# The opening of a two-layer decoder trunk in a fixed order: x in 8 pieces in turn with the weights, a first unit in halves

## The chip, the cores and the metric

The kernel runs on one core of a Trainium2 chip. A core has a matrix engine (TensorE, PE in the profile, with its weight loads shown as PEld), a vector engine (DVE), a scalar engine (ACT), GpSimd (POOL) and an engine that mostly issues transfers (SyncE, SP). Each engine takes its instructions in the order in which they stand in its own stream, and they wait for each other by semaphores. The metric is the device time of one execution in microseconds; the kernel before takes 2566.13 us (median of 3 runs, 2565.7 to 2566.15).

## What is computed

256 tokens of 2048 channels pass through two layers. Layer 0 has a Mamba-2 state-space mixer, layer 1 a short gated convolution, and each is followed by a gated feed-forward with a causal convolution. All is float32. Cut to what the opening computes:

```python
def rms_norm(x, w):
    y = x * lax.rsqrt(jnp.mean(x * x, axis=-1, keepdims=True) + EPS)
    return y * w

def ssd_mixer(u, w_in, conv_w, conv_b, dt_bias, a_log, d_skip, norm_w, w_out):
    zxbcdt = u @ w_in                                  # u: 256 x 2048, w_in: 2048 x 10304
    z, xbc, dt_raw = jnp.split(zxbcdt, [D_INNER, D_INNER + SSM_CONV_DIM], axis=-1)
    xbc = jax.nn.silu(causal_dwconv(xbc, conv_w, conv_b))
    xs, bm, cm = jnp.split(xbc, [D_INNER, D_INNER + SSM_BC_DIM], axis=-1)
    dt = jax.nn.softplus(dt_raw + dt_bias)
    ...

for i in range(2):
    x = x + mixer_i(rms_norm(x, mix_norm_w[i]))        # ssd_mixer, then short_conv_mixer
    x = x + conv_ffn(rms_norm(x, ffn_norm_w[i]))
return rms_norm(x, final_norm_w)
```

## The kernel before

**Tiling.** Channels lie on the 128 partitions and tokens along the free dimension, so x is kept as eight pairs of 128 channels (`xp`, `x_pair`), each 128 x 2 x 256. Float32 products are made from split operands: every weight and every activation is divided into a high and a low part, and three products are summed, high times high, high times low and low times high. A *unit* of weights is 2 x 128 rows by 512 columns (`KU`, `COLS`, 512 KB). For each unit ACT casts it to its high part `wh` (L260) and DVE subtracts to get the low part `wl` (L261). The activations' parts lie side by side in an `hl` tile, made by `split_pair` (ACT L206, DVE L207); the first norm's per-channel weight is multiplied in there.

**Streams.** `stream` (L274) makes 512 output columns from all 16 row blocks, eight units in turn. For each unit it goes through four column tiles t and two row blocks k; each of these eight pairs (t, k) has three products, 24 per unit (L293, L294, L297 where one sum is kept in 256 columns). A stream fills two PSUM tiles (`main`, of which there are three) and then evacuates them. The order of streams is B and C of four groups, then for each group xs and z, then the output product, and so on. Weights move on through four raw buffers (`rawpool`) and four buffers each of `wh` and `wl` (`WB`); other PSUM results use two `aux` tiles.

**The opening.** Rows of x are loaded on SP in eight transfers of 256 KB, each 128 tokens by 512 channels (`load_x`, L81). `x_pair` (L367), called ahead of each unit of the first stream, transposes two channel blocks on PE (four transposes, L375), copies them out of PSUM (L380: DVE for the first two pairs, ACT for the others), splits them and adds a sum of squares on DVE (L388). After the eighth pair it also transposes parameter rows 1 to 3 and makes the norm's per-token factor: reduction (L396), Newton steps (`rsqrt`, L158 to L166), a diagonal (L174), a broadcast by four products (L176) and a copy into `r0` (L400). Every evacuation of the first streams multiplies by `r0` (L314), and a convolution along tokens follows (L328, L330). Between the first and second stream stand the products for dt (64 small products, L449), its softplus, running sums, and the row `cs_d` that is written to DRAM (L495) and read back as `cbc` for the decays (L542). Parameter rows are loaded on ACT's queue and transposed (`load_params`, L136); row 0 holds the mixer norm's weights that the first splits need.

**What sets the order.** The program is traced in the order of the code, and a planner then arranges each engine's stream by its own forecast of when each instruction is ready; priority goes by the traced order, and tiles are handed out as buffers come free. `tc.high_priority(0)` moves the splits of the first eight units ahead (L259). Nine products of ones (L97), read by nobody, run before x arrives.

Of the kernel before, what the change touches and what calls it, by code (L numbers as in the profile page):

```python
# [16 lines left out]
P = 128  # L17
T = 256
# [21 lines left out]
def trunk_kernel(ctx, tc, a, out):  # L40
# [35 lines left out]
    tokpool = start.enter_context(tc.tile_pool(name="tokpool", bufs=2))  # L76
    xt = []
    for c in range(2):
        xt.append(tokpool.tile([P, D], F32, tag="xt", name=uid("xt")))

    def load_x(q):  # L81
        for c in range(2):
            nc.sync.dma_start(
                out=xt[c][:, q * 512 : (q + 1) * 512],
                in_=a["x"][0, c * P : (c + 1) * P, q * 512 : (q + 1) * 512],
            )

# [48 lines left out]
    def load_params(i):  # L136
        n = min(P, total - i * P) if i else n_mix
        rt = small.tile([P, P], F32, tag="prow", name=uid("prow"))
        for off, r in pieces[i]:
            nc.scalar.dma_start(out=rt[off : off + r.shape[0], :], in_=r)  # L140
        ps = aux()
        nc.tensor.transpose(ps[:, :n], rt[:n, :], ident[:n, :n])
        nc.vector.tensor_copy(prm[i][:, :n], ps[:, :n])
# [6 lines left out]
    load_params(0)  # L150

# [1 line left out]
    def rsqrt(v, n):  # L153
        """v**-0.5 for v > 0, [P, n], from an integer seed by Newton's method."""
        r = small.tile([P, n], F32, tag="rs_r", name=uid("rs_r"))
        t = small.tile([P, n], F32, tag="rs_t", name=uid("rs_t"))
        sh = small.tile([P, n], I32, tag="rs_i", name=uid("rs_i"))
        ts(out=sh, in0=v.bitcast(I32), scalar1=1, scalar2=None, op0=ALU.logical_shift_right)  # L158
        ts(
            out=r.bitcast(I32), in0=sh, scalar1=-1.0, scalar2=float(0x5F3759DF),  # L160
            op0=ALU.mult, op1=ALU.add,
        )
        for _ in range(3):
            stt(out=t, in0=r, scalar=-0.5, in1=v, op0=ALU.mult, op1=ALU.mult)
            tt(out=t, in0=t, in1=r, op=ALU.mult)
            stt(out=r, in0=t, scalar=1.5, in1=r, op0=ALU.add, op1=ALU.mult)  # L166
        return r

    def bcast_tok(r):
        """r [tokens, 2] -> PSUM [P, 256], the same row on every partition."""  # L170
        dg = small.tile([P, 2, P], F32, tag="dg", name=uid("dg"))
        ps = aux()
        for c in range(2):
            ts(out=dg[:, c, :], in0=ident, scalar1=r[:, c : c + 1], scalar2=None, op0=ALU.mult)  # L174
        for c in range(2):
            mm(ps[:, c * P : (c + 1) * P], ones, dg[:, c, :], start=True, stop=True)  # L176
# [21 lines left out]
    def split_pair(hl, src, wname=None, k0=0):  # L198
        """hl[:, j] = [high | low] parts of src[:, j] (times a per-channel weight)."""
# [4 lines left out]
        for j in range(2):  # L204
            w = pcol(wname, k0 + j)
            act(hl[:, j, 0:T], src[:, j, :], AF.Copy, scale=w)  # L206
            stt(  # L207
                out=hl[:, j, T : 2 * T], in0=src[:, j, :], scalar=w,
                in1=hl[:, j, 0:T].bitcast(F32), op0=ALU.mult, op1=ALU.subtract,
            )  # L210

# [35 lines left out]
    units = []  # L247
    taken = [0]

    def load_unit():  # L250
        w, c0, kc = plan[len(units)]
        raw = rawpool.tile([P, KU, COLS], F32, tag="raw", name=uid("raw"))
        nc.sync.dma_start(
            out=raw,
            in_=w[kc * P : (kc + KU) * P, c0 : c0 + COLS].rearrange("(k p) n -> p k n", p=P),
        )
        wh = wpool.tile([P, KU, COLS], F32R, tag="wh", name=uid("wh"))
        wl = wpool.tile([P, KU, COLS], F32R, tag="wl", name=uid("wl"))
        with tc.high_priority(0 if len(units) < NKD // KU else None):  # L259
            nc.scalar.copy(wh, raw)  # L260
            tt(out=wl, in0=raw, in1=wh.bitcast(F32), op=ALU.subtract)  # L261
# [12 lines left out]
    def stream(c0, hls, kcs, evac, one=False, before=None):  # L274
        """Products of COLS columns of w with the split activations; evac(pair, psum).

        The sum lies in columns 0..T of psum, or with one unset in two parts, 0..T and T..2T.
        """
        pts = [psm.tile([P, 2, 512], F32, tag="main", name=uid("main")) for _ in range(2)]
        n = len(kcs)  # L280
        for u in range(0, n, KU):
            if before is not None:
                before(u)
            wh, wl = weight_unit(c0, kcs[u], WB - 1 if before is None else 1)
            for t in range(4):
                o = pts[t // 2][:, t % 2, :]
                for k in range(KU):
                    i = u + k
                    hl = hls[i // 2][:, i % 2, :]
                    lw = slice(t * P, (t + 1) * P)  # L290
                    first, last = i == 0, i == n - 1
                    if one:
                        mm(o[:, 0:T], wh[:, k, lw], hl[:, 0:T], start=first, stop=False)  # L293
                        mm(o[:, 0:T], wh[:, k, lw], hl[:, T : 2 * T], start=False, stop=False)  # L294
                    else:
                        mm(o, wh[:, k, lw], hl, start=first, stop=False)  # L296
                    mm(o[:, 0:T], wl[:, k, lw], hl[:, 0:T], start=False, stop=last)  # L297
# [22 lines left out]
    def conv(s, width, wname, nk, k0, bname=None, tag="tp", pool=None):  # L320
        """Causal depthwise conv along tokens; channels k0*128.. of nk*128."""
# [15 lines left out]
    class Norm:  # L337
        """Sum of squares over channels, gathered pair by pair."""
# [24 lines left out]
    xp, xhl = [], []  # L363
    ss = small.tile([P, 2, 4], F32, tag="ss", name="ss")
    first = {}

    def x_pair(u):  # L367
        m = u // KU
        if m % 2 == 1 and m < 7:
            load_x(m // 2 + 1)  # L370
        ps = aux()
        for j in range(2):
            for c in range(2):
                k = 2 * m + j
                nc.tensor.transpose(  # L375
                    ps[:, j * T + c * P : j * T + (c + 1) * P], xt[c][:, k * P : (k + 1) * P], ident
                )
        t = xpool.tile([P, 2, T], F32, tag="x", name=uid("x"))
        copy = nc.vector.tensor_copy if m < 2 else nc.scalar.copy
        copy(t, ps.rearrange("p (j t) -> p j t", j=2))  # L380
        xp.append(t)
        h = new_hl()
        split_pair(h, t, "mix", 2 * m)
        xhl.append(h)
        q, c = divmod(m, 2)
        sq = tmp.tile([P, 512], F32, tag="tp", name=uid("tp"))
        piece = xt[c][:, q * 512 : (q + 1) * 512]
        stt(  # L388
            out=sq, in0=piece, scalar=1.0, in1=piece, op0=ALU.mult, op1=ALU.mult,
            accum_out=ss[:, c, q : q + 1],  # L390
        )
        if m == NKD // 2 - 1:
            for i in range(1, 4):
                load_params(i)
# [6 lines left out]
            first["r0"] = r0  # L401

    NCX = CONVD // P

    def bc_stream(g, o, before=None):
        """B (o = 0) or C (o = 1) of groups g..g+3."""
# [12 lines left out]
    bs = bc_stream(0, 0, x_pair)  # L419
    r_tok, r0 = first["r_tok"], first["r0"]  # L420

# [1 line left out]
    dtw = tokpool.tile([P, NKD, NH], F32, tag="dtw", name="dtw", bufs=1)  # L423
    nc.sync.dma_start(
        out=dtw, in_=s_in[:, DI + CONVD :].rearrange("(k p) h -> p k h", p=P)
    )
    i0, o0 = divmod(base["mix"], P)
    tt(
        out=dtw, in0=dtw,
        in1=prm[i0][:, o0 : o0 + NKD].unsqueeze(2).to_broadcast([P, NKD, NH]), op=ALU.mult,  # L430
    )
    def row_bcast(src, n, tag):
        t = tokpool.tile([P, n], F32, tag=tag, name=tag, bufs=1)
        nc.scalar.dma_start(out=t, in_=src.partition_broadcast(P))
# [4 lines left out]
    d_bc = row_bcast(a["ssd_d"][0], NH, "d_bc")  # L439
    dch = cpool.tile([P, NH // 2], F32, tag="dch", name="dch")  # L440
    for hh in range(2):
        nc.vector.tensor_copy(
            dch[hh * 64 : (hh + 1) * 64, :],
            d_bc[hh * 64 : (hh + 1) * 64, :].rearrange("p (j h) -> p h j", h=2)[:, hh, :],
        )
# [19 lines left out]
    act(na, alog_bc, AF.Exp)  # L465
# [31 lines left out]
    for i in range(4, nrt):  # L497
        load_params(i)
# [128 lines left out]
    def residual_stream(hls, kcs, norm, nhl, nname, one=False):  # L627
        """x += products; when norm is given, x is final: gather its norm, split it."""
# [220 lines left out]
```

## Time and profile before

| what | value |
|---|---|
| median of 3 runs | 2566.13 us |
| profiled execution, span from first to last instruction | 2563.7 us |
| granted PE clock, mean | 0.998 |
| idle time of PE put down to x's transfers | 3.4 us, 3 times, longest 2.5 |
| idle time of PE put down to a copy of parameters | 1.6 us, once |
| units' transfers of 512 KB, median from issue to landing | 3.6 to 4.6 us |

The span leaves out what lies around the first and last instruction. In the timeline a row gives start, duration, engine, line, operation, output and input tiles and how many alike were merged; in brackets stands the idle time before and what ended it. Durations of PE overlap, since products are pipelined: the distance between starts tells its pace.

### The profile page before, as it was taken

To read this page: it belongs to the slowest core of one execution; us is meant where nothing else is said; L and a number is where in the kernel's file an instruction comes from. 1 tells how busy PE (TensorE), PEld (TensorE's weight loads), DVE (VectorE), ACT (ScalarE), POOL (GpSimd) and SP (SyncE) were. 2 spreads that over 40 slices of the span, in tenths; PEclk is the share of its full clock that TensorE was granted. 3 is DMA by queue.
4 is the path that set the end of the run, shared out by engine and by line. 5 is a ranking of instruction groups with operands and counts; after the bars stand their busy time and mean duration, and the time that the engine had idled before them with its cause. 6 is when DMAs were issued, how large, how long until landed. Compare 5 with 4: busy or idle time off the path is not lost.

```text
span 2563.7 us, 38305 instructions
## 1 busy us (share of the span) xinstructions
PE 2545.1 (99%) x15101; PEld 2234.2 (87%) x15101; DVE 1790.0 (70%) x2600; ACT 1311.8 (51%) x1620; POOL 1.1 (0%) x8
## 2 busy tenths in 40 slices
PE   9999999999999999999999999999999999999998
PEld 8899998998888888888888888888888888888886
DVE  7788875788777776557776666666677764577764
ACT  5565543566555554345555444444555553455543
POOL 0000000000000000000000000000000000000000
PEclk9999999999999999999999999999999999999999
DMA  6666656665656555655555656566555566655564
GB/s 210 188 182 196 186 174 185 190 185 169 197 182 194 189 188 181 191 188 185 193 189 182 195 184 186 184 195 189 175 184 187 187 196 192 193 187 188 187 192 143
DMA packets 254696, 478.76 MB, mean 187 GB/s; under 512 B 17651, under 2 KB 27059, under 8 KB 254387
## 3 DMA queue, kind: packets, MB, share of 16 engines
q1 hardware_dynamic: 251856, 473.49, 59.0%
q10 hardware_dynamic: 2659, 2.82, 0.3%
q8 instruction: 118, 1.93, 0.3%
q14 instruction: 63, 0.52, 0.1%
HBM read 474.09 MB, written 2.16 MB: 186 GB/s over the span
## 4 chain that ended last, share of the span: by engine, by line
PE 97%; DMA 1%; DVE 1%; ACT 1%; issue 0%; SPq 0%; ACTq 0%; DVEq 0%
PE main L296 50%; PE main L297 28%; PE main L794 3%; PE main L796 3%; PE main L795 3%; PE main L293 3%; PE main L294 3%; DMA raw<-in_ssd_w_in_dram 1%; PE aux L585 1%; DMA cbc<-cs_d 0%; PE aux L449 0%; PE aux L593 0%; PE aux L566 0%; ACT wh L260 0%; DVE wl L261 0%; PE aux L176 0%
## 5 line engine op out<-in xcount | busy, mean ns | idle before, releaser
L296 PE MATMUL main<-hl,wh 128*128 128x512 f32 x5568 | 1944.3, 396 | 0.2 <-DVE hl L207 0.2
L297 PE MATMUL main<-hl,wl 128*128 128x256 f32 x6336 | 1749.9, 280 | 0.2 <-DVE wl L261 0.2
L261 DVE TENSOR_TENSOR wl<-raw,wh 128x1024 fp32r<-128x1024 f32 x880 | 1073.7, 1224 | 711.1 <-ACT wh L260 710.5
L260 ACT CAST wh<-raw 128x1024 fp32r<-128x1024 f32 x880 | 920.9, 1049 | 1080.6 <-PE main L296 734.4
L296 PEld LDWEIGHTS main<-hl,wh 128*128 128x128 f32 x5568 | 1035.2, 188 | 237.3 <-issue 1.6
L297 PEld LDWEIGHTS main<-hl,wl 128*128 128x128 f32 x6336 | 1196.3, 189 | 15.1 <-issue 1.1
L294 PE MATMUL main<-hl,wh 128*128 128x256 f32 x768 | 217.6, 284 | 0.0
L293 PE MATMUL main<-hl,wh 128*128 128x256 f32 x768 | 217.6, 286 | 0.0
L293 PEld LDWEIGHTS main<-hl,wh 128*128 128x128 f32 x768 | 146.9, 192 | 2.6 <-issue 2.2
L294 PEld LDWEIGHTS main<-hl,wh 128*128 128x128 f32 x768 | 147.4, 192 | 0.6 <-issue 0.6
L794 PE MATMUL main<-wh,hl 128*128 128x512 f32 x352 | 137.8, 392 | 0.8 <-DVE xtok L800 0.8
L796 PE MATMUL main<-wh,hl 128*128 128x512 f32 x352 | 137.7, 391 | 0.0
L795 PE MATMUL main<-wl,hl 128*128 128x512 f32 x352 | 137.6, 391 | 0.0
L330 DVE SCALAR_TENSOR_TENSOR tp<-tp,prm,tp 128x255 f32<-128x255 f32 x208 | 90.6, 477 | 0.0
L306 ACT COPY tp<-main 128x512 f32<-128x512 f32 x128 | 74.3, 581 | 28.9 <-PE main L297 28.9
L308 DVE TENSOR_TENSOR tp<-main,tp 128x512 f32<-128x512 f32 x128 | 87.6, 684 | 0.0
L794 PEld LDWEIGHTS main<-wh,hl 128*128 128x128 f32 x352 | 66.2, 188 | 15.5 <-DVE xtok L800 1.2
L796 PEld LDWEIGHTS main<-wh,hl 128*128 128x128 f32 x352 | 66.2, 188 | 14.5
L795 PEld LDWEIGHTS main<-wl,hl 128*128 128x128 f32 x352 | 66.2, 188 | 14.3
L330 DVE SCALAR_TENSOR_TENSOR g<-tp,prm,g 128x254 f32<-128x254 f32 (+1 forms) x176 | 74.7, 478 | 0.1
L328 ACT ACTIVATE g<-tp,prm,prm 128x256 f32<-128x256 f32 x88 | 48.2, 596 | 38.0 <-DVE tp L317 38.0
L317 DVE TENSOR_TENSOR tp<-tp,rrow 128x512 f32<-128x512 f32 x96 | 66.1, 689 | 1.8
(133 smaller groups left out, 957.8 us busy)
## 6 DMA issues: line engine op xcount, KB each, us to landing
raw<-in_ffn_w_up_dram SPq DMA_DIRECT2D x352, 512.0 KB, 4.1
raw<-in_ffn_w_down_dram SPq DMA_DIRECT2D x176, 512.0 KB, 3.6
raw<-in_ssd_w_in_dram SPq DMA_DIRECT2D x160, 512.0 KB, 4.6
raw<-in_sc_w_in_dram SPq DMA_DIRECT2D x96, 512.0 KB, 4.3
raw<-in_ssd_w_out_dram SPq DMA_DIRECT2D x64, 512.0 KB, 4.0
raw<-in_sc_w_out_dram SPq DMA_DIRECT2D x32, 512.0 KB, 4.3
cbc<-cs_d SPq DMA_DIRECT2D x32, 256.0 KB, 5.4
xt<-in_x_dram SPq DMA_DIRECT2D x8, 256.0 KB, 5.0
```

What stands on the lines that cost most here:

```text
L260: nc.scalar.copy(wh, raw)
L261: tt(out=wl, in0=raw, in1=wh.bitcast(F32), op=ALU.subtract)
L293: mm(o[:, 0:T], wh[:, k, lw], hl[:, 0:T], start=first, stop=False)
L294: mm(o[:, 0:T], wh[:, k, lw], hl[:, T : 2 * T], start=False, stop=False)
L296: mm(o, wh[:, k, lw], hl, start=first, stop=False)
L297: mm(o[:, 0:T], wl[:, k, lw], hl[:, 0:T], start=False, stop=last)
L306: nc.scalar.copy(pb, pt[:, :, T : 2 * T])
L308: tt(out=s, in0=pt[:, :, 0:T], in1=pb, op=ALU.add)
L330: stt(out=y[:, j, d:T], in0=s[:, j, 0 : T - d], scalar=pcol(wname, (width - 1 - d) * nk + k0 + j), in1=y[:, j, d:T], op0=ALU.mult, op1=ALU ...
L794: mm(pt[:, c, :], hi_, wh[:, k, :], start=(i == 0), stop=False)
L795: mm(pt[:, c, :], hi_, wl[:, k, :], start=False, stop=False)
L796: mm(pt[:, c, :], lo_, wh[:, k, :], start=False, stop=(i == n - 1))
```

## The change

x lies in one tile, 128 tokens by 2 halves by 2048 channels, and comes in eight transfers of 256 channels for both halves (256 KB each, 1 KB lines in place of 2 KB). The transfers of x and of the first eight units are written out in turn: x0, unit 0 in two halves, x1, unit 1, x2, unit 2, x3, unit 3, x4, x5, unit 4, x6, unit 5, x7, unit 6, unit 7; then parameter rows 1 to 3 (moved from ACT's queue to SP's, with four buffers in place of two), the dt weights and three broadcast rows. Unit 0 is split in halves, and its products go by k first. Rows 4 and later are loaded on SP as well. An extra copy on ACT reads the ones before x is there.

`pin` (`tc.keep_in_program_order`) ties an instruction behind the one traced before it on its engine: an order of issue, no wait. It is put on everything that the first stream does on SP, PE, ACT and DVE. The x pair of the next unit is now traced behind the second of the eight pairs (t, k) of a unit, and within it the splits of x stand ahead of the splits of that pair's unit. What is traced elsewhere stays with the planner.

```diff
+    xt = tokpool.tile([P, 2, D], F32, tag="xt", name="xt")
+    pin = tc.keep_in_program_order
+    def load_x(m):
+        pin(nc.sync.dma_start(
+            out=xt[:, :, m * T : (m + 1) * T],
+            in_=a["x"][0, :, m * T : (m + 1) * T].rearrange("(c p) d -> p c d", p=P),
+        ))
...
+    spare = small.tile([P, 1], F32, tag="spare", name="spare")
+    pin(nc.scalar.copy(spare, ones[:, 0:1]))
...
     def load_params(i):
-        rt = small.tile([P, P], F32, tag="prow", name=uid("prow"))
+        rt = small.tile([P, P], F32, tag="prow", name=uid("prow"), bufs=4)
         for off, r in pieces[i]:
-            nc.scalar.dma_start(out=rt[off : off + r.shape[0], :], in_=r)
+            if i:
+                pin(nc.sync.dma_start(out=rt[off : off + r.shape[0], :], in_=r))
+            else:
+                nc.scalar.dma_start(out=rt[off : off + r.shape[0], :], in_=r)
+        return rt, n
...
     def load_unit():
...
+        def half(ks, put):
+            put(nc.scalar.copy(wh[:, ks, :], raw[:, ks, :]))
+            put(tt(
+                out=wl[:, ks, :], in0=raw[:, ks, :], in1=wh[:, ks, :].bitcast(F32),
+                op=ALU.subtract,
+            ))
+        if i == 0:
+            return half
+        with tc.high_priority(0 if i < NKD // KU else None):
+            half(slice(0, KU), pin if i < NKD // KU else lambda ins: ins)
...
     def stream(c0, hls, kcs, evac, one=False, before=None):
...
+            order = [(t, k) for t in range(4) for k in range(KU)]
+            if before is not None and u == 0:
+                before(0)
+                order.sort(key=lambda tk: tk[1])
+            wh, wl = weight_unit(c0, kcs[u], WB - 1 if before is None else 0)
+            for at, (t, k) in enumerate(order):
+                if before is not None and at == 2 and u + KU < n:
+                    before(u // KU + 1)
...
+        if before is not None:
+            before(n // KU)
...
+    def x_pair(m):
+        if m == NKD // 2:
             for i in range(1, 4):
-                load_params(i)
+                turn_params(i, *prows[i - 1], pin)
...
+        for j in range(2):
+            for c in range(2):
+                k = 2 * m + j
+                pin(nc.tensor.transpose(
+                    ps[:, j * T + c * P : j * T + (c + 1) * P], xt[:, c, k * P : (k + 1) * P], ident
+                ))
+        t = xpool.tile([P, 2, T], F32, tag="x", name=uid("x"))
+        copy = nc.vector.tensor_copy if m < 2 else nc.scalar.copy
+        pin(copy(t, ps.rearrange("p (j t) -> p j t", j=2)))
...
+        if m == 0:
+            turn_params(0, *prow0, pin)
+            half = load_unit()
+            half(slice(0, 1), pin)
+        split_pair(h, t, "mix", 2 * m, pin)
+        if m == 0:
+            half(slice(1, 2), pin)
+        else:
+            load_unit()
+        for c in range(2) if m % 2 else ():
...
+            pin(stt(
+                out=sq, in0=piece, scalar=1.0, in1=piece, op0=ALU.mult, op1=ALU.mult,
+                accum_out=ss[:, c, m // 2 : m // 2 + 1],
+            ))
...
+    load_raw()
+    for m in range(1, 4):
+        load_x(m)
+        load_raw()
+    load_x(4)
+    for m in range(5, NKD // 2):
+        load_x(m)
+        load_raw()
+    load_raw()
+    prows += [load_params(i) for i in range(1, 4)]
```

`turn_params` holds the transpose and copy that stood in `load_params`; `load_raw` issues the transfer of the next unit, in two halves for unit 0. The dt weights' scaling, two copies of the skip factors and one exponential behind the first stream are pinned too.

More of the change, by code (lines that the diff above doesn't have):

```diff
@@ L75, in trunk_kernel @@
     start = ExitStack()
[L76 to L86, printed above, removed]
+    tokpool = start.enter_context(tc.tile_pool(name="tokpool", bufs=1))
+    xt = tokpool.tile([P, 2, D], F32, tag="xt", name="xt")
[5 more added lines that the diff above has]
+        ))
     ident = cpool.tile([P, P], F32, tag="ident", name="ident")
@@ L245, in trunk_kernel, with load_raw @@
     planned_ffn(1)
-    units = []
+    raws, units = [], []
     taken = [0]
-    def load_unit():
[L251 to L256, printed above, removed]
+    def load_raw():
+        i = len(raws)
+        w, c0, kc = plan[i]
+        raw = rawpool.tile([P, KU, COLS], F32, tag="raw", name=uid("raw"))
+        for k in range(0, KU, 1 if i == 0 else KU):
+            n = 1 if i == 0 else KU
+            ins = nc.sync.dma_start(
+                out=raw[:, k : k + n, :],
+                in_=w[(kc + k) * P : (kc + k + n) * P, c0 : c0 + COLS].rearrange(
+                    "(k p) n -> p k n", p=P
+                ),
+            )
+            if i < NKD // KU:
+                pin(ins)
+        raws.append(raw)
+    def load_unit():
+        i = len(units)
+        if i == len(raws):
+            load_raw()
+        raw, raws[i] = raws[i], None
         wh = wpool.tile([P, KU, COLS], F32R, tag="wh", name=uid("wh"))
         wl = wpool.tile([P, KU, COLS], F32R, tag="wl", name=uid("wl"))
-        with tc.high_priority(0 if len(units) < NKD // KU else None):
-            nc.scalar.copy(wh, raw)
-            tt(out=wl, in0=raw, in1=wh.bitcast(F32), op=ALU.subtract)
         units.append((wh, wl))
+        def half(ks, put):
[8 more added lines that the diff above has]
+            half(slice(0, KU), pin if i < NKD // KU else lambda ins: ins)
     def weight_unit(c0, kc, ahead=WB - 1):
@@ L365, in trunk_kernel @@
     first = {}
[L367 to L392, printed above, removed]
+    prows = []
+    def x_pair(m):
+        if m == NKD // 2:
             for i in range(1, 4):
-                load_params(i)
+                turn_params(i, *prows[i - 1], pin)
             sst = small.tile([P, 2], F32, tag="sst", name="sst")
@@ L417, in bc_stream @@
         return res
[L419 to L420 removed]
+    load_raw()
[6 more added lines that the diff above has]
+        load_raw()
+    load_raw()
+    prows += [load_params(i) for i in range(1, 4)]
     dtw = tokpool.tile([P, NKD, NH], F32, tag="dtw", name="dtw", bufs=1)
[L424 removed]
+    pin(nc.sync.dma_start(
         out=dtw, in_=s_in[:, DI + CONVD :].rearrange("(k p) h -> p k h", p=P)
[L426 to L431, printed above, removed]
+    ))
     def row_bcast(src, n, tag):
         t = tokpool.tile([P, n], F32, tag=tag, name=tag, bufs=1)
[L434 removed]
+        pin(nc.sync.dma_start(out=t, in_=src.partition_broadcast(P)))
         return t
@@ L439, in trunk_kernel @@
     d_bc = row_bcast(a["ssd_d"][0], NH, "d_bc")
+    bs = bc_stream(0, 0, x_pair)
+    r_tok, r0 = first["r_tok"], first["r0"]
+    i0, o0 = divmod(base["mix"], P)
+    pin(tt(
+        out=dtw, in0=dtw,
+        in1=prm[i0][:, o0 : o0 + NKD].unsqueeze(2).to_broadcast([P, NKD, NH]), op=ALU.mult,
+    ))
     dch = cpool.tile([P, NH // 2], F32, tag="dch", name="dch")
     for hh in range(2):
-        nc.vector.tensor_copy(
+        pin(nc.vector.tensor_copy(
             dch[hh * 64 : (hh + 1) * 64, :],
             d_bc[hh * 64 : (hh + 1) * 64, :].rearrange("p (j h) -> p h j", h=2)[:, hh, :],
-        )
+        ))
     ps = aux()
```

52 lines of the change are left out of this document (28 added, 24 removed).

## The prediction

> **What bounds the kernel now.** I read the head of the page first, then busy times by stretch (PE, weight loads, DVE, ACT, POOL, granted clock, DMA share, GB/s), then PE's groups and the timeline of the opening.
>
> ```profile
> span 2563.7 us, 38305 instructions
> PE 2545.1 (99%) x15101; PEld 2234.2 (87%) x15101; DVE 1790.0 (70%) x2600; ACT 1311.8 (51%) x1620; POOL 1.1 (0%) x8
> ```
> ```profile
> 0.00:5.00 5.00, 3.95 (x18) 3.91 (x18) 1.17 (x5) 0.07 (x1) 1.10 (x8) 1.00 0.51 148
> 5.00:10.00 5.00, 2.31 (x14) 1.61 (x13) 4.03 (x9) 3.94 (x5) 0.00 (x0) 0.88 1.02 361
> ...
> 20.00:30.00 10.00, 9.91 (x84) 9.70 (x83) 10.00 (x24) 9.20 (x17) 0.00 (x0) 1.00 0.91 288
> ```
>
> PE is busy 99% of the span, so only stretches in which it has nothing to do can be won or lost. They lie mainly in the opening: in the first 5 us all 18 PE instructions are idle-time products that nothing reads, and in the next 5 it is busy 2.31 us. From 20 us on it is full (9.91 of 10). The question is therefore how much PE work is done by the time the opening ends, not how early it begins. I count it for the kernel before:
>
> ```profile
> L294 PE MATMUL main<-hl,wh 128*128 128x256 f32 x72 | 20.4, 289 | 0.0
> L293 PE MATMUL main<-hl,wh 128*128 128x256 f32 x73 | 20.3, 290 | 0.0
> L297 PE MATMUL main<-hl,wl 128*128 128x256 f32 x72 | 19.8, 287 | 0.0
> L375 PE MATMUL aux<-ident,xt 128*128 128x128 f32 x32 | 5.8, 316 | 3.6 <-DMA xt<-in_x_dram 3.4 <-DVE prm L143 0.2
> ...
> L142 PE MATMUL aux<-ident,prow 128*128 128x128 f32 x3 | 0.7, 282 | 0.6 <-DMA prow<-in_ffn_conv_b_dram 0.6
> L142 PE MATMUL aux<-ident,prow 32*128 32x32 f32 x1 | 0.3, 311 | 0.0
> ```
> ```profile
> 14.16 0.28 PE L293 MATMUL main<-hl,wh 128*128 128x256 f32 x1
> ...
> 14.28 0.28 PE L294 MATMUL main<-hl,wh 128*128 128x256 f32 x1
> ...
> 42.06 0.61 PE L176 MATMUL aux<-dg,ones 128*128 128x128 f32 x4
> 42.51 7.26 PE L449 MATMUL aux<-dtw,x 128*128 128x64 f32 x64
> ```
>
> The first block groups PE up to 42.05 us, the second is its timeline. Dense products start 0.12 us apart (14.16, 14.28). By 42.06, where the first norm's row is broadcast (L176), PE has done 72+73+72 = 217 products and 36 transposes; at 0.12 each (transposes taken alike) that is 30.4 us of work. So 42.06 - 30.4 = **11.7 us were lost**, and directly behind it 64 other products run without a gap.
>
> **The change part by part.** x comes in 8 pieces of 256 KB instead of 4 times 2; the first unit's weights come, are split and multiplied in halves; parameter rows 1 to 3 and the later ones move from ACT's queue to SP's; and what the first stream does is pinned in program order on SP, PE, ACT and DVE.
>
> The start gains. Rows for it:
>
> ```profile
> 4.59 0.69 DVE L388 SCALAR_TENSOR_TENSOR tp<-xt 128x512 f32<-128x512 f32 x1 [2.54 <-DMA xt<-in_x_dram]
> 4.93 1.28 ACT L260 ACT_TABLE_LOAD   x1 [4.93 <-DMA xt<-in_x_dram]
> ...
> 6.30 0.66 PE L375 MATMUL aux<-ident,xt 128*128 128x128 f32 x4 [0.21 <-DVE prm L143]
> ...
> 7.00 0.69 DVE L380 COPY x<-aux 128x512 f32<-128x512 f32 x1 [0.15 <-PE aux L375]
> 7.27 1.04 ACT L260 CAST wh<-raw 128x1024 fp32r<-128x1024 f32 x1 [1.05 <-DMA raw<-in_ssd_w_in_dram]
> 8.25 0.51 ACT L206 ACTIVATE hl<-x,prm 128x256 fp32r<-128x256 f32 x1
> 8.35 1.23 DVE L261 TENSOR_TENSOR wl<-raw,wh 128x1024 fp32r<-128x1024 f32 x1 [0.66 <-ACT wh L260]
> 8.67 0.49 ACT L206 ACTIVATE hl<-x,prm 128x256 fp32r<-128x256 f32 x1
> 9.07 1.03 ACT L260 CAST wh<-raw 128x1024 fp32r<-128x1024 f32 x1
> ```
> ```profile
> 6.06 0.19 DVE L143 COPY prm<-aux 128x32 f32<-128x32 f32 x1
> ...
> 10.10 0.88 DVE L207 SCALAR_TENSOR_TENSOR hl<-x,prm,hl 128x256 fp32r<-128x256 f32 x2
> ```
>
> The first 256 KB of x had landed at 4.59; the new first piece is as large and issued first, and now carries both token halves, so its transposes start at 4.6. The copy of x starts 0.70 us behind them (6.30 to 7.00): 5.3, done 6.0. Parameter copy 0.19: 6.2. First high half 0.51: 6.7. On DVE the half subtraction stands in front: by the 0.69 of rows with 512 columns it runs 6.2 to 6.9, then the first low half, 0.88/2 = 0.44, to 7.35. Then five products of 0.12 and at 7.95 the transposes of x pair 1. The half cast fits in ACT before x is copied, because the spare copy brings the table load (1.28, at 4.93) forward; without it the cast would end near 6.8, about where it is needed. That is an earlier start than before, by some 2 us.
>
> Then comes what costs. Behind the first two of a unit's eight pairs (t, k), six products, program order puts the transposes of the next x pair. Now pinned: on ACT copy of x, two high halves, **then** the cast of the next weights; on DVE low halves, **then** the weights' subtraction. The cast needs only weights that landed long ago, but in line it waits for x's copy, which waits for the transposes, which wait for the six products of the unit before, which need that unit's subtraction. It is a ring:
>
> ```profile
> L380 ACT COPY x<-aux 128x512 f32<-128x512 f32 x6 | 3.3, 588 | 0.3 <-PE aux L375 0.3
> ...
> L261 DVE TENSOR_TENSOR wl<-raw,wh 128x1024 fp32r<-128x1024 f32 x16 | 19.4, 1215 | 2.2 <-ACT wh L260 2.2
> ```
>
> transposes to copy 0.70; copy 0.59; two high halves 0.82 (8.25 to 9.07, where the cast behind them starts); cast 1.05; to the subtraction 0.04 (7.27+1.04 = 8.31 to 8.35); subtraction 1.22; to PE 0.05, an estimate after that 0.04; the third product of the unit and three more, 0.48. Sum **4.95 us a unit**. PE's own work per unit is 24 products and 4 transposes, 28 x 0.12 = 3.36. So PE stands 1.6 us in each. Unit 1 first: transposes at 7.95, copy (still DVE, 0.69) ends 9.34, +0.82+1.05+0.04+1.22+0.05 = 12.5. Unit 7's subtraction: 12.5 + 6 x 4.95 = 42.2. Its other 22 products end at 44.85, three parameter transposes at 45.2.
>
> Next the norm. Behind unit 7's subtraction stand two sums of squares (0.69 each, 43.6), then the norm's chain:
>
> ```profile
> 36.88 0.15 DVE L164 SCALAR_TENSOR_TENSOR rs_t<-rs_r,var 128x2 f32<-128x2 f32 x1
> 37.07 0.16 DVE L165 TENSOR_TENSOR rs_t<-rs_t,rs_r 128x2 f32<-128x2 f32 x1
> ...
> 39.69 0.48 DVE L174 TENSOR_SCALAR dg<-ident,rs_r 128x128 f32<-128x128 f32 x2
> ```
> ```profile
> 42.70 0.37 ACT L400 COPY rrow<-aux 128x256 f32<-128x256 f32 x1 [2.27 <-PE aux L176]
> ...
> 43.11 1.29 DVE L314 TENSOR_TENSOR tp<-main,rrow 128x512 f32<-128x512 f32 x2 [1.41 <-ACT rrow L400]
> ...
> 44.47 4.91 DVE L330 SCALAR_TENSOR_TENSOR bc<-tp,prm,bc 128x255 f32<-128x255 f32 x12
> ```
>
> 13 small steps 0.19 apart (2.5), 0.48: broadcast at 46.6 against 42.06. From there to the first freed PSUM tile 42.06 to 43.11 plus half of 1.29: 1.7, so 48.3. By then PE has done 192 + 32 + 4 + 4 = 232 instructions, 27.9 us: lost 20.4 us, less what fills its gaps. Only products of the second stream can: one free PSUM tile takes half a unit (12 products, 1.44 us), and four weight buffers allow at most four such, 5.8 us, the first when unit 4 is through (about 30). Ends: 20.4 - 5.8 = 14.6, which is **+2.9** against 11.7; no fill, **+8.7**. I take three halves (4.3), since the fourth's weights come only behind unit 7, and one weight subtraction of 1.22 inside the norm's chain: 20.4 + 1.2 - 4.3 = 17.3, **+5.6**.
>
> What moves at nothing: the DMAs. Pieces and weights up to unit 7 are 6 MB, at the 288 to 361 GB/s of the rows above some 20 us, and the ring asks for them over 42. Rows 1 to 3 (eight transfers) now queue on SP behind weights that wait for a raw buffer, but are used only at 45. Rows 5 to 7 stand in SP's queue until the transposes at 45.2 free their buffers, and weights behind them wait too; the units ahead are 3 x 24 x 0.12 = 8.6 us of PE work, so that hides it, and a longer wait would be paid one for one. If this cover went (pieces with 1 KB lines at half the rate), x pair 1 would land near 8.5 instead of before 7.95, +0.6. The weights for dt are now scaled behind the first evacuation on DVE, whose convolution runs 4.91 us, so dt's 64 products start near 55 instead of 42.5. They are not missed by PE at once, but the decays come late.
>
> ```profile
> 68.57 0.36 ACTq L495 DMA_DIRECT2D cs_d<-cst  x1
> ...
> 83.15 0.33 PE L142 MATMUL aux<-ident,prow 128*128 128x128 f32 x1 [1.64 <-DVE prm L143]
> ```
>
> The write at 68.57 comes near 81. I bound that with the only stall that DVE causes there: -1.6 if the parameter copies, now early, take it away, +3 if it comes twice more; I take 0, as both have a cause. So 2563.7 + 5.6 = 2569.3, and the median lies 2566.1 - 2563.7 = 2.4 above the span: **2572**.
>
> The clock, by rows:
>
> ```profile
> 8.50:9.00 0.50, 0.00 (x0) 0.00 (x0) 0.50 (x1) 0.50 (x2) 0.00 (x0) 0.82 1.21 360
> 9.00:9.50 0.50, 0.06 (x1) 0.09 (x2) 0.50 (x2) 0.50 (x2) 0.00 (x0) 0.50 0.79 274
> ...
> 12.00:12.50 0.50, 0.50 (x6) 0.50 (x5) 0.50 (x1) 0.50 (x2) 0.00 (x0) 0.77 0.81 259
> 12.50:13.00 0.50, 0.50 (x7) 0.50 (x6) 0.50 (x2) 0.50 (x1) 0.00 (x0) 1.00 0.49 173
> ```
>
> PE was idle from 6.96 (6.30+0.66), and by 9.0 it ran at half clock, for about 3.4 us. So here less than 2 us of standing was enough, with a thin load before it. The Trainium skill ("TensorE: Matmul & The Clock Gate", HAM oscillation) says that gaps over about 3.4 us bring the low clock; by that rule the ring's gaps of 1.6 us would cost nothing more, while this trace leaves it open.
>
> **The rivals.**
> *Not slower.* The second stream fills all four halves (+2.9), and the stall at 83 goes (-1.6): +1.3, 2567.4. It decides at 3.6 us of fill with an uninterrupted norm chain: from there the loss is under 5.1 us (20.4 - 3.6 - 11.7). For it: the planner filled just so before (217 products by 42.06, with only 192 in the stream). Against: the fourth half comes too late.
> *Half clock in the ring.* In each unit the on-ring PE part doubles (0.48, and 0.5 for transposes): +1 per throttled unit, three units +3: 2575.
> *The ring is not closed* (the order does not come out as I read it, casts run ahead): PE-bound, unit 7 ends at 7.35 + 8 x 3.36 = 34.2, loss 7.35 - 0.6 = 6.8 and about 1 at the norm, -4; with the 83 stall -5.6: 2560.5. For it: only that ACT and DVE, at 0.59 + 0.82 + 1.05 and 0.88 + 1.22 + 0.69 a unit, could keep up.
>
> **How the numbers follow.** About 0.2%, 5.1 us, is what a measurement of this kernel can tell from no change. Ring with part fill 0.50 (a tenth of that inside 0.2%), not slower 0.36, half clock 0.07, open ring 0.07 (a seventh of it inside). Slower 0.45 + 0.07 = 0.52; same 0.05 + 0.36 + 0.01 = 0.42; faster 0.06. The range takes the not-slower case with the -1.6 to -2 beyond it and, above, no fill (+8.7) with part of the late decays: 2565 to 2577. The forecast's own range is 2570 to 2575.
>
> **What would show it.** Right: the first product before 7.5 us; transposes of x about 4.95 us apart; PE waiting for the subtraction (L261's successor) six or seven times for 1 to 1.6 us, on ACT the cast directly behind the high halves; unit 7 ending near 45; the broadcast at 46 to 48; dt's products near 55. Wrong: transposes 3.4 us apart (ring open), or casts ahead of x's copy; the clock at 0.5 after 15 us (rival three); products in the gaps before unit 4 is through.

## The result, and the profile after

| | before | after |
|---|---|---|
| median, us | 2565.70 (6 runs, 2564.56 to 2566.15) | 2573.21 (6 runs, 2572.59 to 2575.89) |
| ratio to before, 95% interval | | 1.0032 [1.0022, 1.0042] |
| profiled execution: span / its time | 2563.7 / 2566.15 | 2573.4 / 2575.14 |

The change costs 0.32% [0.22%, 0.42%], about 7.5 us. The head of the page of after:

```profile
span 2573.4 us, 38324 instructions
PE 2547.6 (99%) x15101; PEld 2235.6 (87%) x15101; DVE 1790.3 (70%) x2601; ACT 1321.2 (51%) x1630; POOL 1.1 (0%) x8
```

PE executes the same 15101 instructions; its busy time grew by 2.5 us and the span by 9.7, so most of the loss is idle time. Busy times by stretch of after (columns as in the prediction) show where:

```profile
5.00:10.00 5.00, 3.62 (x20) 3.14 (x19) 3.63 (x7) 1.87 (x5) 0.00 (x0) 0.79 0.98 307
...
20.00:30.00 10.00, 7.69 (x58) 6.87 (x58) 5.44 (x10) 4.88 (x9) 0.00 (x0) 1.00 0.51 148
```

Before 10 us PE does more than before the change (20 instructions instead of 14 in the second stretch), but from 20 to 30 us it is busy 7.69 of 10 where it was 9.91, with 58 instructions instead of 84. One turn of that stretch, from the timeline of after (start, duration, engine, line, operation, tiles, in brackets the idle time before and what ended it):

```profile
18.66 0.60 PE L420 MATMUL aux<-ident,xt 128*128 128x128 f32 x4
...
19.30 0.59 ACT L425 COPY x<-aux 128x512 f32<-128x512 f32 x1 [2.53 <-PE aux L420]
...
19.92 0.91 ACT L213 ACTIVATE hl<-x,prm 128x256 fp32r<-128x256 f32 x2
...
20.73 1.03 ACT L283 CAST wh<-raw 128x1024 fp32r<-128x1024 f32 x1
...
21.80 1.23 DVE L284 TENSOR_TENSOR wl<-raw,wh 128x1024 fp32r<-128x1024 f32 x1 [0.45 <-ACT wh L283]
21.82 0.39 PE L327 MATMUL main<-hl,wh 128*128 128x256 f32 x1 [0.40 <-ACT wh L283]
...
23.08 0.39 PE L331 MATMUL main<-hl,wl 128*128 128x256 f32 x1 [0.76 <-DVE wl L284]
...
23.66 0.60 PE L420 MATMUL aux<-ident,xt 128*128 128x128 f32 x4
```

Read it as a circle. Transposes at 18.66 (L420, four merged); ACT, idle for 2.53 us until they end, copies x at 19.30, makes the high halves at 19.92 and only then casts the next weights at 20.73; DVE subtracts at 21.80; at 23.08 PE has the low part it needs, and the next transposes stand at 23.66. From 18.66 to 23.66 are 5.00 us, while PE has 28 instructions of 0.12 us in it. All three engines wait in every turn (PE twice, 0.40 us for the high part and 0.76 for the low part): none of them is full.

Behind the first stream comes the second loss. PE's groups up to 54.5 us, then DVE, ACT and PE behind unit 7:

```profile
L327 PE MATMUL main<-hl,wh 128*128 128x256 f32 x80 | 24.6, 307 | 4.1 <-ACT wh L283 2.9 <-ACT hl L213 1.2
L331 PE MATMUL main<-hl,wl 128*128 128x256 f32 x80 | 23.9, 300 | 4.3 <-DVE wl L284 4.3
L328 PE MATMUL main<-hl,wh 128*128 128x256 f32 x80 | 23.2, 290 | 0.1
```
```profile
41.76 1.23 DVE L284 TENSOR_TENSOR wl<-raw,wh 128x1024 fp32r<-128x1024 f32 x1 [0.45 <-DMA prow<-in_ffn_conv_b_dram]
...
44.13 2.35 DVE L284 TENSOR_TENSOR wl<-raw,wh 128x1024 fp32r<-128x1024 f32 x2
46.40 0.15 DVE L409 TENSOR_REDUCE sst<-ss 128x2 f32<-128x8 f32 x1
46.47 1.22 DVE L284 TENSOR_TENSOR wl<-raw,wh 128x1024 fp32r<-128x1024 f32 x1
47.60 0.48 DVE L150 COPY prm<-aux 128x128 f32<-128x128 f32 x2
...
48.07 1.22 DVE L284 TENSOR_TENSOR wl<-raw,wh 128x1024 fp32r<-128x1024 f32 x1
...
50.61 0.29 DVE L150 COPY prm<-aux 128x128 f32<-128x128 f32 x1 [0.65 <-PE aux L149]
...
52.18 0.48 DVE L181 TENSOR_SCALAR dg<-ident,rs_r 128x128 f32<-128x128 f32 x2
```
```profile
40.70 3.88 ACT L283 CAST wh<-raw 128x1024 fp32r<-128x1024 f32 x4
```
```profile
52.52 0.71 PE L183 MATMUL aux<-dg,ones 128*128 128x128 f32 x4 [0.75 <-DVE dg L181]
54.52 0.36 PE L327 MATMUL main<-hl,wh 128*128 128x256 f32 x1 [1.28 <-DVE tp L350]
```

ACT casts the weights of units 7 to 10 in one go from 40.70 (unit 11's follow), and so four subtractions of the second stream (44.13 twice, 46.47, 48.07) fall into the norm's chain on DVE. Three parameter copies stand in it as well, the last with a wait of 0.65 for its transpose, and the chain reaches its diagonal only at 52.18. PE broadcasts at 52.52 and has its next product at 54.52. By then it has done 240 products, 36 transposes (counted as in the prediction) and 4 for the broadcast, 33.6 us at 0.12: **20.9 us lost, against 11.7 before**, 9.2 more. Further on, one wait has gone and one is new: the stall of 1.64 at 83 us has no row in after, and this one, in PE's groups of after from 55 to 200 us, has come:

```profile
L331 PE MATMUL main<-hl,wl 128*128 128x256 f32 x341 | 95.6, 286 | 2.4 <-DVE wl L284 2.4
```

9.2 + 2.4 - 1.6 = 10.0, against 9.7 between the two spans. The medians differ by 7.5, since the profiled execution of after lies 1.9 above its median.

### The profile page after: what moved, and what is told of

Same layout as the page of the kernel before. It is cut to its first block, busy times and chain, and to the rows that moved or that the text cites. A ratio compares the mean times of both kernels' runs of the same rounds, so it can differ in the third digit from the quotient of the medians.

```text
span 2573.4 us, 38324 instructions
## 1 busy us (share of the span) xinstructions
PE 2547.6 (99%) x15101; PEld 2235.6 (87%) x15101; DVE 1790.3 (70%) x2601; ACT 1321.2 (51%) x1630; POOL 1.1 (0%) x8
## 4 chain that ended last, share of the span: by engine, by line
PE 97%; DVE 1%; ACT 1%; issue 0%; DMA 0%; SPq 0%; ACTq 0%
PE main L330 50%; PE main L331 29%; PE main L327 3%; PE main L328 3%; PE main L848 3%; PE main L849 3%; PE main L850 3%; PE aux L639 1%; DVE wl L284 0%; ACT wh L283 0%; PE aux L647 0%; PE aux L503 0%; PE aux L620 0%; PE aux L183 0%; PE aux L190 0%
## 5 line engine op out<-in xcount | busy, mean ns | idle before, releaser
L284 DVE TENSOR_TENSOR wl<-raw,wh 128x1024 fp32r<-128x1024 f32 (+1 forms) x881 | 1072.9, 1222 | 704.8 <-ACT wh L283 703.0
L283 ACT CAST wh<-raw 128x1024 fp32r<-128x1024 f32 (+1 forms) x881 | 920.5, 1048 | 1066.2 <-PE main L330 733.2
```

The lines of the kernel that those rows point to most:

```text
L283: put(nc.scalar.copy(wh[:, ks, :], raw[:, ks, :]))
L284: put(tt(out=wl[:, ks, :], in0=raw[:, ks, :], in1=wh[:, ks, :].bitcast(F32), op=ALU.subtract,))
```

## The experiments

All ratios are to the kernel before, run on the same chip beside each experiment; these chips differ, and the median of the kernel before lay between 2565.70 and 2567.23 on them. "Lost" is the opening's lost PE work in the profiled execution, counted as above, at the first product behind the broadcast. Edits are to the changed kernel unless another is named.

| kernel | what differs from after | median, us | ratio, 95% interval | lost, us |
|---|---|---|---|---|
| after | | 2573.21 | 1.0032 [1.0022, 1.0042] | 20.9 |
| e14_transfers | transfers of units 8 to 11 ahead of the late rows | 2573.27 | 1.0025 [1.0016, 1.0035] | 21.0 |
| e1_cast_first | cast and subtraction ahead of x's copy and splits | 2570.28 | 1.0016 [1.0007, 1.0024] | 18.3 |
| e8_second_units | e1 and transfers of units 8 and 9 | 2566.74 | 1.0002 [0.9993, 1.001] | 16.3 |
| e13_lookahead | x pairs one unit earlier, order kept, transfers of 8 and 9 | 2567.91 | 1.0005 [0.9996, 1.0014] | 15.7 |
| e7_dt_behind_norm | dt weights scaled right behind the norm | 2573.22 | 1.0038 [1.0024, 1.0052] | 20.3 |
| e9_all | e8 and e7 | 2566.80 | 1.0001 [0.9992, 1.001] | 14.8 |
| e10_all_u1 | e9, for pair 1 x's copy ahead of cast and subtraction | 2565.09 | 0.9998 [0.9989, 1.0006] | 12.6 |
| e11_raw_first | e10 and transfers of units 10 and 11 | 2561.07 | 0.9979 [0.997, 0.9988] | 10.9 |
| e3_dt_free | work for dt not pinned | 2577.46 | 1.0046 [1.0034, 1.0059] | 23.5 |
| e6_a_c | e1 and e3 | 2573.53 | 1.003 [1.0019, 1.0041] | 18.4 |
| e4_sp_only | pins on SP alone | 2567.75 | 1.0005 [0.9996, 1.0014] | 16.1 |
| e12_sp_only_rows | e4, late rows back on ACT's queue | 2566.57 | 0.9997 [0.9988, 1.0006] | 16.1 |

(By the broadcast PE has done 214 products in e4 and 208 in e12, and 240 in the others.) The lost work holds one thing that no edit aimed at: products that follow each other at 0.21 us instead of 0.12 in the first 14 us (last section). There are about 12 such steps in after, 2 in e1, 18 in e8 and 20 in e11, worth some 1.1, 0.2, 1.7 and 1.9 us. So differences of lost work below 2 us do not show what an edit did.

**The ring opened.** In `x_pair`, the splits of the weights go ahead of the transposes and what follows them:

```diff
+        if 0 < m < NKD // 2:
+            load_unit()
...
         for j in range(2):
             for c in range(2):
...
         split_pair(h, t, "mix", 2 * m, pin)
         if m == 0:
             half(slice(1, 2), pin)
-        else:
-            load_unit()
```

> The only edit: in each x pair after the first, the cast and the subtraction of the unit's weights stand ahead of the pair's transposes, copy and splits instead of behind them. Ring theory: the ring loses cast and subtraction (2.3 us) and is shorter than PE's own 3.4 us a unit, so transposes of x come 3.4 to 3.6 us apart instead of 4.99, PE's waits for subtractions in units 2 to 7 vanish, the first stream ends near 36 to 37 us instead of 45, the broadcast comes 7 to 9 us earlier, and the median falls by 6 to 9 us, to 2564 to 2567. Rival (the loss lies in the norm's chain and in the late dt, the ring only fills up what would be waited there anyway): the transposes come closer, but the median falls by under 3 us, to 2570 or more.

The ring opened as expected: in the middle of the stream the transposes stand 3.31 us apart.

```profile
20.82 0.60 PE L422 MATMUL aux<-ident,xt 128*128 128x128 f32 x4
...
24.13 0.60 PE L422 MATMUL aux<-ident,xt 128*128 128x128 f32 x4
```

But the time fell by only 2.9 us. That is the number of the rival, not of the ring theory. ACT's and PE's timelines of e1 give another reason for it than the rival's:

```profile
35.46 1.04 ACT L283 CAST wh<-raw 128x1024 fp32r<-128x1024 f32 x1 [4.91 <-DMA raw<-in_ssd_w_in_dram]
36.41 0.58 ACT L427 COPY x<-aux 128x512 f32<-128x512 f32 x1
```
```profile
33.23 0.28 PE L331 MATMUL main<-hl,wl 128*128 128x256 f32 x1
36.55 0.38 PE L327 MATMUL main<-hl,wh 128*128 128x256 f32 x1 [3.05 <-ACT wh L283]
```

The cast at 35.46 is unit 8's: not pinned, and put by the planner ahead of the copy of x pair 7. Its weights stood on SP's queue behind the parameter rows, the dt weights and three broadcast rows, the last of which is the row for `d_bc`:

```profile
25.91 0.43 SPq L479 DMA_DIRECT2D d_bc<-in_ssd_d_dram  x1
26.44 4.45 SPq L263 DMA_DIRECT2D raw<-in_ssd_w_in_dram  x3
```

So ACT waits 4.91 us at the head of its line for a transfer issued at 26.44 or later, x's copy waits behind it, and PE stands for 3.05. The queue itself is slow there: from 27 to 31 us all DMA engines together move 12 to 26 GB/s, and the 32 KB row for `d_bc` takes 8.2 us from issue to landing; why was not traced. The lateness then reaches the norm: its chain on DVE stands 2.99 us, until 46.61, for parameter transposes that PE does behind unit 7. With the ring gone, a queue that it had hidden is late next.

**That queue mended, with the ring and without.** `e8_second_units` adds two transfers to e1 (`load_raw()` twice behind unit 7's, pinned); `e14_transfers` adds the transfers of units 8 to 11 to the changed kernel and leaves its ring closed:

```diff
     load_raw()
+    load_raw()
+    load_raw()
     prows += [load_params(i) for i in range(1, 4)]
```

(e14 and e11 have two more behind the last line.)

> The ring opened as in the first run (casts ahead of x's copy), and the transfers of units 8 and 9 pinned directly behind unit 7's, ahead of the parameter rows, the dt weights and the broadcast rows. Theory: in the first run the planner had put unit 8's cast ahead of x pair 7's copy, and it waited 4.9 us for a transfer that stood behind twelve others; now it does not wait, the eighth x pair's transposes and unit 7 follow at 3.3 us like the others, the first stream ends near 37 us instead of 41, and the median falls by 3 to 5 us from 2570.3, to 2565 to 2567. Rival (transfers are limited by the raw buffers, not by their order): the wait stays, within 1 us of 2570.

> The changed kernel with nothing altered but the transfers: those of units 8 to 11 are pinned ahead of the late rows (8 and 9 right behind unit 7's, 10 and 11 behind the parameter rows), as in e11_raw_first; casts stay behind the splits and the dt weights' scaling stays where the change put it. Theory (the ring of one unit is what costs; early transfers alone are no use, because the second stream's casts still come behind the ring on ACT): transposes of x 4.9 to 5.0 us apart, 2570.5 to 2573.5. Rival (the ring is harmless when the second stream's weights are there to fill its gaps): products of the second stream before 35 us, 2561 to 2566.

Transfers alone give nothing: in e14 the transposes stay 4.99 apart, and the lost work is after's.

```profile
18.68 0.60 PE L420 MATMUL aux<-ident,xt 128*128 128x128 f32 x4
...
23.67 0.60 PE L420 MATMUL aux<-ident,xt 128*128 128x128 f32 x4
```

The weights of unit 8 are there, but their cast still stands in line behind unit 7's, so the gaps stay empty. With the ring open two such transfers are worth 3.5 us by the medians (e1 to e8; the intervals just overlap), and both together take back nearly all of the change's loss. The two gains need each other: open ring alone 0.16 of a per cent, transfers alone nothing that the intervals separate, both 0.30.

**Is it the ring, or the place of the cast?** `e13_lookahead` keeps the cast behind the splits and instead calls each x pair one unit earlier (pair 1 beside pair 0), so that the circle has two units' time. It has e8's two transfers as well:

```diff
-                if before is not None and at == 2 and u + KU < n:
-                    before(u // KU + 1)
+                if before is not None and at == 2 and u + 2 * KU < n:
+                    before(u // KU + 2)
```

> The order of the changed kernel is kept within each x pair (cast and subtraction behind the splits), but every pair is traced one unit earlier, so that the ring spans two units; and the transfers of units 8 and 9 are pinned behind unit 7's, as in e8_second_units. Theory (it is the closed ring of one unit that costs, not the place of the cast as such): transposes of x 3.3 to 3.5 us apart, first stream through by 38 to 39, 2565 to 2568, as e8. Rival (the order of casts behind splits costs by itself, or the pair ahead takes PE's time too early): transposes 4 to 5 us apart, 2570 to 2573.

```profile
21.57 0.60 PE L421 MATMUL aux<-ident,xt 128*128 128x128 f32 x4
...
24.88 0.60 PE L421 MATMUL aux<-ident,xt 128*128 128x128 f32 x4
```

3.31 us apart, as in e1, with another cure, and a time like e8's, where e14, with the transfers and the closed circle, stays at 2573.27: what costs is the closed circle of one unit, not the cast's place as such.

**The late dt.** `e7_dt_behind_norm` pins the scaling of the dt weights on DVE right behind the norm's diagonal, ahead of the evacuation.

> The only edit to the changed kernel: the pinned scaling of the dt weights stands directly behind the norm's diagonal on DVE, ahead of the first evacuation, instead of behind its convolution; it waits for nothing that is late there. The ring is as in the changed kernel (4.99 us). Theory (late dt is a loss of its own beside the ring): dt's 64 products come at about 53 instead of 67.9 us and fill the hole of 1.3 us behind the broadcast; the decays come some 14 us earlier, so PE's wait of 2.4 us near 117 goes: 2 to 4 us below the changed kernel, 2569 to 2571. Rival (dt's place does not matter, or another stall takes the room): within 1 us of 2573.

The 64 products start at 53.87 us instead of 67.90, the wait of 2.4 is gone from the profile, and a parameter copy is waited for elsewhere (1.4 us); the median is the same. Its expectation fell: late dt has no price of its own that the median shows. The evidence is coarse, though: two of e7's five runs took over 2579 us, and the interval of its ratio is 7 us wide. `e3_dt_free` and `e6_a_c` take the pins off that work instead (the scaling, the copies to `dch`, the exponential).

> The only edit: the scaling of the dt weights, the two copies of the skip factors and the exponential behind the first stream are no longer pinned. Theory (late dt is a loss of its own): the scaling moves into DVE's idle time in the ring, dt's 64 products come by 55 us instead of 68, the decays come some 12 us earlier, PE's wait of 2.4 us for a subtraction near 117 us goes, and the hole of 1.3 us behind the broadcast is filled: 2 to 4 us less, 2569 to 2571. Rival (the ring alone makes the loss): within 1 us of the changed kernel's 2573.

> Both edits of the first two runs of this call: weights' splits ahead of x's, and the dt work unpinned. If ring and late dt are separate losses, their gains add: 8 to 12 us below the changed kernel, 2561 to 2565, so a little faster than the kernel before (2565.7), since the first product comes some 2 us earlier. If late dt was only a consequence of the ring, it equals the first run of this call within 1 us.

Both turned out the opposite way: by the medians 4.3 us slower than after, and 3.3 slower than e1, with intervals that just overlap. DVE's timeline of e3, and ACT's and DVE's of e6:

```profile
38.66 0.37 DVE L496 COPY dch<-d_bc 64x32 f32<-64x32 f32 x2 [2.09 <-DMA d_bc<-in_ssd_d_dram]
```
```profile
31.75 0.26 ACT L519 ACTIVATE na<-alog_bc 128x64 f32<-128x64 f32 x1 [3.69 <-DMA alog_bc<-in_ssd_a_log_dram]
```
```profile
34.30 0.36 DVE L496 COPY dch<-d_bc 64x32 f32<-64x32 f32 x2 [4.59 <-DMA d_bc<-in_ssd_d_dram]
```

The planner put small instructions that nobody needs yet into the opening, ahead of x's copies and splits, and there they wait 2 to 4.6 us for rows that are late on SP's queue. It is the same fault as e1's cast of unit 8. In e3 two turns of the ring take 6.2 us instead of 5.0, and the lost work is 2.6 us above after's. In e6 these waits only take the place of e1's (18.4 us lost against 18.3), so what makes e6 slower than e1 lies behind the opening: there PE waits twice for parameter copies, 1.9 and 1.8 us, where e1 has one wait of 1.1. By the medians, the pins on that work, which the change added, are worth having.

**No order on the engines at all.** `e4_sp_only` makes `pin` do nothing except on SP; `e12_sp_only_rows` also puts parameter rows and broadcast rows back on ACT's queue.

> The only edit: the pins act on SP alone; PE, ACT and DVE are ordered by the planner again, with x in 8 pieces and the transfers in their fixed order. Theory (the compute order costs, the transfers' order does not): no ring, transposes not at a fixed distance, 2560 to 2567, so no slower than the kernel before. Rival (the transfers cost: parameter rows on SP behind weights, 1 KB lines): it stays at 2570 or more.

> As e4_sp_only (pins on SP alone, the planner orders PE, ACT and DVE), with the parameter rows and the three broadcast rows back on ACT's queue as before the change; the dt weights stay on SP. Theory (what e4 still loses comes from instructions that the planner put ahead and that wait for late rows): e4's waits at 5.9 to 9.0, 30.6 to 32.6 and 33.1 to 36.2 us shrink, broadcast near 42 to 44, 2562 to 2566. Rival (the pieces of x and their turn among the weights cost that by themselves): 2567 to 2568.5 as e4.

e4 takes back 5.5 of the 7.5 us: the fixed order of the engines, not the pieces of x, holds most of the loss. PE's holes in e4 are of the kind just seen: ACT stands 6.24 us for a broadcast row, until 31.76, with x's copy and high halves behind it, and DVE 5.04 us for another, until 34.58, with low halves behind it.

```profile
31.76 0.26 ACT L521 ACTIVATE na<-alog_bc 128x64 f32<-128x64 f32 x1 [6.24 <-DMA alog_bc<-in_ssd_a_log_dram]
```
```profile
32.55 0.33 PE L151 MATMUL aux<-ident,prow 128*128 128x128 f32 x1 [1.36 <-ACT x L427]
...
36.18 0.47 PE L330 MATMUL main<-hl,wh 128*128 128x256 f32 x1 [2.59 <-DVE hl L216]
```

In e12 these are gone, yet its time differs from e4's by no more than the intervals: it has waits for x's own pieces (3.7 us before transposes, from the groups of its profile) instead, with the rows on a second queue beside them. Both theories were half right.

**All together.** `e9_all` is e8 with e7's edit; `e10_all_u1` puts x's copy of pair 1 alone ahead of the cast and the subtraction, since on DVE it stood behind the subtraction until 11.11 us in e9; `e11_raw_first` moves units 10 and 11 ahead of the dt weights.

> Both edits of this call's first two runs. If the three losses (ring, late second weights, late dt) are separate, the gains add: 2561 to 2564, some 2 to 4 us below the kernel before (2565.7). If late dt only hurts while the ring delays everything, it equals the second run of this call within 1 us.

> As the run before it, and for x pair 1 alone (whose copy is on DVE) the copy stands ahead of the unit's cast and subtraction, which in the first run held the copy back until 11.6 us. Unit 1's first product about 12.2 instead of 12.9: 0.5 to 1 us below the run before it; if the start of unit 1 is bound by the weights' transfer, no difference.

> The transfers of units 10 and 11 are pinned ahead of the dt weights and the broadcast rows, on top of e10_all_u1. Theory (the cast of unit 10 waits for a transfer that stands behind rows on SP's queue): PE's wait of 1.7 to 2.8 us for a high part near 40 us goes; the broadcast of the first norm at 44 to 45 instead of 45.7; 2562 to 2564, about 2 us below the kernel before. Rival (the wait is PE's slack in another place and what is behind takes it up): as e10, 2565 +- 0.7.

e9 gains nothing over e8 by the medians, e10 1.7 us over e9 with overlapping intervals. e10 still waited 1.7 us for unit 10's cast; with its transfer ahead that wait is gone, the ratio falls from 0.9998 to 0.9979, and the time of 2561.07 lies below both kernels: **0.21% [0.12%, 0.30%] under before, 12 us under after**. ACT and PE of e11:

```profile
30.08 2.93 ACT L283 CAST wh<-raw 128x1024 fp32r<-128x1024 f32 x3
```
```profile
43.65 0.61 PE L183 MATMUL aux<-dg,ones 128*128 128x128 f32 x4
44.54 1.66 PE L509 MATMUL aux<-dtw,x 128*128 128x64 f32 x13 [0.28 <-DVE dtw L415]
```

Three casts, unit 7's and two of the second stream's, follow each other without a wait where e1 stood for 4.91, beside the first stream's products, and the broadcast comes at 43.65 with 240 products done, against 42.06 with 217 before. Lost work: 44.54 - 33.6 = 10.9. That is 10.0 us less than after by this count, of 12.1 in the medians; the rest was not traced. Against the kernel before, the count gives 0.8 us (10.9 against 11.7) of the 2.5 between the two profiled spans, 2561.2 and 2563.7, so most of what makes e11 faster than before stays open. Which of e10's smaller edits e11 needs was not tried singly.

## Why the prediction was right, step by step

**The forecast was 2572, "ring with part fill"; 2573.21 came, and by that mechanism.** Two of its sizes were off, in opposite directions, and they do not cancel: the prediction added 5.6 us to the span, the profile shows 9.7. That the median still came within 1.2 us is in part luck. The forecast took the median 2.4 above the span, and in the profiled execution of after its time is 1.7 above it; and that execution lies 1.9 above its median, which a forecast could not know.

*The start.* Forecast: transposes at 4.6, of pair 1 at 7.95. Rows of after:

```profile
4.79 0.60 PE L420 MATMUL aux<-ident,xt 128*128 128x128 f32 x4
...
8.11 1.05 PE L420 MATMUL aux<-ident,xt 128*128 128x128 f32 x4
...
9.61 0.41 PE L327 MATMUL main<-hl,wh 128*128 128x256 f32 x1
9.82 0.41 PE L328 MATMUL main<-hl,wh 128*128 128x256 f32 x1
```

Right to 0.2 us. Products here stand 0.21 apart (9.61, 9.82), which the forecast had at 0.12.

*The ring, 4.95 a unit.* Measured 4.99 to 5.00, term by term from the turn shown: transposes to copy 0.64 (0.70), copy 0.62 (0.59), high halves 0.81 (0.82), cast and handing on 1.07 (1.09), subtraction and on to PE 1.28 (1.27), products 0.58 (0.48). Unit 7's subtraction was to be through at 42.2: it starts at 41.76 and runs 1.23, so 43.0. The prediction's sign was a wait of 1 to 1.6 us for the subtraction; it came as two waits, 0.40 for the cast and 0.76 for the subtraction, while the pace lost per turn, 5.00 - 3.36 = 1.6 us, is as forecast. That the ring carries the loss is shown by e8 and e13, which open it in two ways and leave 0.02 to 0.05% of the 0.32%, against e14, which leaves it closed and keeps the loss. Opened alone (e1) it gives only 2.9 us, since the late queue takes the rest.

*Part fill, three half units.* Four came (240 products, less 192 of the first stream), 1.4 us better than forecast; but none in the ring's gaps, as the forecast had it from unit 4 on: all behind unit 7, for their casts start with that at 40.70.

***The mis-sized step: "one weight subtraction of 1.22 inside the norm's chain", broadcast at 47.8.*** There were four, with two parameter copies (0.48) between them and a third behind a wait of 0.65, and it came at 52.52: 4.7 us late. 17.3 + 4.7 - 1.4 = 20.6, against the 20.9 measured. It is the price of the fill itself: whoever counts on four half units must also count the DVE work that makes their weights, and where it stands in line.

*Late dt, taken at nothing, bounds -1.6 to +3.* dt's products came at 67.90 (forecast 55). Both things that the bound allowed for came at once, the stall at 83 gone and a new wait of 2.4: +0.8 in the profile, and by e7 nothing in the median.

*Transfers at nothing.* True in this kernel, and for the reason given, the ring as cover. The price without that cover was put at 0.6, at x pair 1; e1 shows it elsewhere and larger: 4.91 us on ACT for unit 8's weights. The forecast went through SP's queue but didn't ask what an unpinned instruction does that waits for its last entries.

*The rivals.* "Not slower" needed 3.6 us of fill with an uninterrupted norm chain: it had the fill (5.8 us) and not the chain. "Half clock in the ring" did not come: the granted clock is 1.00 from 20 to 30 us with gaps of 0.40 and 0.76 in each turn. Products there also stand 0.12 apart. The rule quoted from the Trainium skill ("TensorE: Matmul & The Clock Gate", HAM oscillation) holds for these gaps. It does not hold for a wait of 3.05 us in e1, which is shorter than the rule's about 3.4 us and still brought the low clock (last section); there the measurement decides. "The ring is not closed", 2560.5: with the ring opened by hand the time is 2570.3, 2566.7 with two transfers in time as well, and 2561.1 in e11, which has four and the smaller edits of e10; the rival had the size of the ring right but left the queue out.

## What to carry to other kernels

When an order is fixed by hand, walk once around it: if work that needs only long-landed data (a cast of weights) stands behind work that waits for the engine it feeds, the engines take turns instead of overlapping, and the sum of one turn, read from single durations, gives the pace. Look at the unpinned neighbours and the transfers together: an in-order engine stands at its head, so a small instruction whose row is last on the queue can hold up the whole opening, and fixing order without transfers, or transfers without order, gives a part of the gain or none. Work brought forward to fill gaps has a cost on the engine that prepares it, and the place of that cost decides.

## What was not expected of the hardware

**The same standing, two clocks.** In e1 and e11 the opening is alike up to the first product: both have it at 7.54 us after a wait of 1.18.

```profile
7.54 0.38 PE L327 MATMUL main<-hl,wh 128*128 128x256 f32 x1 [1.18 <-ACT hl L213]
...
8.40 0.28 PE L327 MATMUL main<-hl,wh 128*128 128x256 f32 x1
8.52 0.28 PE L328 MATMUL main<-hl,wh 128*128 128x256 f32 x1
```
```profile
8.65 0.41 PE L327 MATMUL main<-hl,wh 128*128 128x256 f32 x1
8.86 0.41 PE L328 MATMUL main<-hl,wh 128*128 128x256 f32 x1
...
13.98 0.33 PE L327 MATMUL main<-hl,wh 128*128 128x256 f32 x1
```

In e1 (first block) products go on at 0.12, in e11 at 0.21 until 13.98, though the granted clock in e11's stretches from 8 to 14 us reads 1.00. PE's work in these 5.3 us took 5.3 x (1 - 0.12/0.21) = 2.3 us longer than at 0.12; how much of it a wait would have taken up otherwise (e1 waits 1.42 us before 12.92) is not shown. The profiled execution of e11 lies 1.95 above its median; that this is why was not shown. The traces of e3 and e8 have the same slow pace from 8.44 on, also under a column of 1.00, while in after, from 9 to 11 us, the column reads 0.50 beside it. The Trainium skill ("TensorE: Matmul & The Clock Gate", What's actually happening) says that the window over which activity is watched runs freely, so that the same kernel has different counts of slow products from run to run; these two openings, though of two kernels, agree with it. The Trainium skill warns on the same page ("TensorE: Matmul & The Clock Gate", Seeing it yourself) that recorded clock events can be unreliable, and e11's column looks like such a case.

**A longer standing did bring the low clock.** Stretches of e1 behind its wait of 3.05 us (granted clock third from the right):

```profile
36.00:39.00 3.00, 1.69 (x7) 1.49 (x8) 2.25 (x2) 3.00 (x6) 0.00 (x0) 0.67 0.70 250
39.00:42.00 3.00, 3.00 (x16) 3.00 (x15) 3.00 (x8) 0.68 (x1) 0.00 (x0) 0.50 0.77 233
```

PE last issued at 33.23; from 39 to 42 us the granted clock is 0.50, and 16 instructions take the 3 us in which 25 would fit at 0.12. So this wait cost PE about 1 us more in this stretch alone. In e10 less was enough: behind waits of 1.70 us (until 39.98) and 0.76 its clock reads 0.55 from 42 to 45 us. The ring's gaps of 0.40 and 0.76 in every 5 us left the clock at 1.00.
